# First loads of a two-layer backbone kernel: two small transfers issued by ScalarE, and eight products on a tile of ones ahead of the first projections

## The chip, the cores and the metric

One Trainium2 chip; the kernel runs on one core, in one launch. The metric is the device time of the launch in microseconds (us). Three runs of the kernel before gave 1178.02, 1180.78 and 1184.63 us; the median is 1180.78 us. One further execution was profiled.

## The reference

A two-layer backbone over 256 latent and 256 context tokens of width 1024, in float32. Every sub-layer is modulated by shift, scale and gate vectors that come from the conditions c and c_ctx. Layer 0 mixes tokens by bidirectional retention, layer 1 by neighbourhood attention; each is followed by a SwiGLU. What matters here is the very start:

```
cond_lat = silu(c);  cond_ctx = silu(c_ctx)
m = split(cond @ ada_w[i] + ada_b[i], 6)          # shift, scale, gate, ... per stream
a = h * (1 + m[1]) + m[0]                         # modulate
q, k, v, g = split(a @ ret_w_in, ...)             # first projections of layer 0
```

## The kernel before

All matrix products are made in float32 precision: mostly as three products on operands split into a high and a low part of type fp32r (`mm3`, L138 to L142). Only the first projections of head 0 start on whole, unsplit float32 operands, so that they need not wait for the split.

The start is written out by hand. `tc.manual_schedule(engines=REG)` (L372 to L424) fixes the order of TensorE (PE), VectorE (DVE), ScalarE (ACT), GpSimd (POOL) and SyncE (SP) in the order of the code. Past it, engines outside later hand-ordered regions take their order from the planner that builds the program on simulated times (`schedule_with_timeline_sim=True`). In the hand-ordered stretch:

- `load_cond` (L162 to L168): SP loads c, spread over all 128 partitions, into `condb[0]`, and c_ctx as a column tile `ccol` (128x8). ACT applies SiLU to both, `ccol` first.
- `load_adab` (L182 to L187): SP loads the adaLN biases `adab_sb` (128x96); POOL adds 1 to the columns of the scales.
- `ada.load_to(2)`, `load_x(0)`, `stream.load_to(1)`: SP loads the first two 512 KB tiles of the transposed adaLN weights (`adaraw`), the first 256 KB tile of tokens (`xt`, the inputs transposed) and the first 512 KB unit of projection weights (`raw`).
- `spread_cond` (L170 to L180): DVE splits `ccol` into `chi` and `clo`; PE spreads them over all partitions by 16 products with the identity, into two PSUM banks; ACT copies the two banks to `condb[1]`.
- Then a loop over eight row blocks kt of the model width. SP loads the next tiles; DVE makes scale and shift columns of kt for each of the two token streams s by multiply-and-sum over `adaraw` and `condb[s]` (L225, 128x1024, two for each kt and s); ACT writes the modulated tokens `am` (L408, 128x256) and their high part (L413); PE multiplies `am` with the unit. For kt below 5 that is `whole_products` (L345 to L354): for each s, four products into the banks of q and k and two into the banks of v, each of which the profile shows as two records. For kt from 5 on the products are split ones (`split_products`, L356 to L369).

PE takes its instructions in the order of the code, so what stands ahead of `whole_products` runs ahead of it. The eight PSUM banks are handed out in turn: two to `spread_cond`, then four for q and k, then four for v.

Of the kernel before, what the change touches and what calls it, by code (L numbers as in the profile page):

```python
# [10 lines left out]
BF16 = mybir.dt.bfloat16  # L11
# [7 lines left out]
P = 128  # L19
D = 1024  # L20
# [24 lines left out]
def backbone(ctx: ExitStack, tc: tile.TileContext, wpack, adapack, cond, condcol, xT, xtok, adab, lncol, lnrow,  # L45
             decay, delta, rope, rpb, mask8, out):
    nc = tc.nc
# [31 lines left out]
    def bank(name):  # L79
        return psum.tile([P, 512], F32, tag="bank", name=name)  # L80
# [75 lines left out]
    adab_sb = const.tile([P, 2, 48], F32, name="adab_sb")  # L156

    ccol = const.tile([P, KT], F32, name="ccol")
# [3 lines left out]
    def load_cond():  # L162


        nc.sync.dma_start(condb[0], cond[0:1, :].partition_broadcast(P))
        nc.sync.dma_start(ccol, condcol)
        nc.scalar.activation(ccol, ccol, AF.Silu)
        nc.scalar.activation(condb[0], condb[0], AF.Silu)  # L168

    def spread_cond():  # L170
        nc.vector.tensor_copy(out=chi, in_=ccol)
        nc.vector.tensor_tensor(out=clo, in0=ccol, in1=chi.bitcast(F32), op=ALU.subtract)
        for half in range(2):
            b = bank(f"cond_{half}")
            for i in range(4):
                k = 4 * half + i
                for n, c in enumerate((chi, clo)):
                    nc.tensor.matmul(b[:, i * P:i * P + P], c[:, k:k + 1].to_broadcast([P, P]), identr,
                                     start=i == 0 and n == 0, stop=i == 3 and n == 1)
            nc.scalar.copy(condb[1][:, half * 512:half * 512 + 512], b)  # L180

    def load_adab():  # L182
        nc.sync.dma_start(adab_sb, adab)
        for l in range(2):
            for g in (1, 4):
                sl = adab_sb[:, l, 8 * g:8 * g + 8]
                nc.gpsimd.tensor_scalar(out=sl, in0=sl, scalar1=1.0, scalar2=0.0, op0=ALU.add, op1=ALU.add)  # L187
# [129 lines left out]
    with Phase("ret", "yTh", "yTl", "vh", "vl", "kh", "kl") as rp:  # L317
# [12 lines left out]
                                      name=f"adaraw{i}")  # L330
# [42 lines left out]
        region = tc.manual_schedule(engines=REG)  # L373
        region.__enter__()
        load_cond()
        load_adab()
        ada.load_to(2)

        for i, w in enumerate("qk"):
            stream.place[16 * RET_H - 4 + i] = (rp, w + "h", w + "l", 1)  # L380
        load_x(0)
        stream.load_to(1)
        spread_cond()
        qk_ps = [bank(f"qk0_{f}") for f in range(4)]
        v_ps = [bank(f"v0_{t}") for t in range(4)]
        for kt in range(KT):
# [591 lines left out]
    with Phase("na", "oTh", "oTl", "qs") as ap:  # L978
# [196 lines left out]
        warm = ap.tile([P, 1], F32, name="warm")  # L1175
# [240 lines left out]
```

## Time and profile before

| | |
|---|---|
| median of three runs | 1180.78 us |
| the profiled execution, its own time | 1181.89 us |
| its span, first to last instruction | 1180.1 us |
| PE busy | 1153.0 us (98% of the span) |
| DVE, ACT, POOL busy | 67%, 39%, 25% |
| bytes moved by DMA | 201.72 MB, mean 171 GB/s |

The time of a row counts from the start of the span. PE's records overlap, since products are pipelined: the distance from one start to the next is the pace, not the length of a record. PEld is the loading of the stationary operand. SPq is SyncE's queue, which issues the transfers.

### The profile page before, as it was taken

Reading aid. Unit: us, or ns where it says so; the run is one execution under the profiler, and the core shown is the slowest. Engines: PE = TensorE matmul, PEld = TensorE weight load, DVE = VectorE, ACT = ScalarE, POOL = GpSimd, SP = SyncE. Lnnn points to the kernel's source line nnn. Section 1 sums busy time; section 2 is a strip of 40 time slices with the busy share of each in tenths; the row PEclk is TensorE's granted clock in tenths of the full one; section 3 lists DMA queues with packets and bytes.
Section 4 is the critical chain, followed back from the end, with each engine's and each line's share of the span. In section 5 each row is a group of like instructions: output and inputs, shape, how many; then the busy total and the mean of one; then the engine's idle time right before and its main releaser. Section 6 shows DMA issues by size and latency. Waiting matters only on the chain. (4 is left out here: it accounts for less than half of the span.)

```text
span 1180.1 us, 15314 instructions
## 1 busy us (share of the span) xinstructions
PE 1153.0 (98%) x5670; PEld 959.7 (81%) x5670; DVE 785.8 (67%) x1131; ACT 454.8 (39%) x714; POOL 293.8 (25%) x282
## 2 busy tenths in 40 slices
PE   7999999999999999999999999999998998999997
PEld 5778888888888888888888888887887877888886
DVE  7986957645745588857776576556265577788645
ACT  3582423332433252322122322244254465566530
POOL 0054114104203549100320000026244435300000
PEclk9999999999999999999999999999999999999999
DMA  8755464233434223566555586426587744777650
GB/s 328 262 202 190 175 206 150 90 126 129 133 107 127 88 72 108 181 145 226 178 192 209 168 271 234 139 66 136 160 233 226 204 141 121 238 237 228 206 167 36
DMA packets 70010, 201.72 MB, mean 171 GB/s; under 512 B 14512, under 2 KB 17072, under 8 KB 69936
## 3 DMA queue, kind: packets, MB, share of 16 engines
q1 hardware_dynamic: 69648, 200.23, 53.2%
q8 instruction: 44, 0.72, 0.3%
q10 hardware_dynamic: 288, 0.52, 0.1%
q14 instruction: 30, 0.25, 0.1%
HBM read 187.98 MB, written 2.25 MB: 161 GB/s over the span
## 5 line engine op out<-in xcount | busy, mean ns | idle before, releaser
L124 DVE TENSOR_TENSOR wlo<-raw,whi 128x1024 fp32r<-128x1024 f32 x220 | 291.9, 1332 | 210.6 <-ACT whi L123 204.0
L123 ACT CAST whi<-raw 128x1024 fp32r<-128x1024 f32 x220 | 229.5, 1048 | 457.5 <-PE f L141 118.1
L225 DVE CUSTOM_DVE_ANT_0 junk<-adaraw,cond,adab_sb 128x1024 bf16<-128x1024 f32 x160 | 219.1, 1369 | 46.9 <-DMA adaraw<-in_adapack 44.5
L141 PE MATMUL f<-aT,whi 128*128 128x512 f32 (+1 forms) x384 | 142.8, 372 | 1.8 <-DVE aT L756 1.7
L142 PE MATMUL f<-aT,wlo 128*128 128x512 f32 (+1 forms) x384 | 142.5, 371 | 0.0
L140 PE MATMUL f<-aT,whi 128*128 128x512 f32 (+1 forms) x384 | 142.5, 372 | 0.0
L857 PE MATMUL f<-aT,whi 128*128 128x512 f32 x320 | 112.9, 397 | 0.0
L313 POOL TENSOR_TENSOR pb_n<-pa_n,mhalf 128x1 f32<-128x1 f32 x12 | 8.4, 704 | 347.8 <-DVE pa_n L312 347.8
L858 PE MATMUL f<-aT,wlo 128*128 128x256 f32 x320 | 90.0, 282 | 0.3 <-DVE wlo L124 0.3
L141 PEld LDWEIGHTS f<-aT,whi 128*128 128x128 f32 x384 | 72.3, 188 | 14.6 <-DVE aT L756 1.9
L142 PEld LDWEIGHTS f<-aT,wlo 128*128 128x128 f32 x384 | 72.3, 188 | 12.6
L140 PEld LDWEIGHTS f<-aT,whi 128*128 128x128 f32 x384 | 72.3, 188 | 12.4
L857 PEld LDWEIGHTS f<-aT,whi 128*128 128x128 f32 x320 | 60.0, 188 | 14.4
L140 PE MATMUL d<-whi,hh 128*128 128x512 f32 x176 | 68.6, 389 | 0.0
L142 PE MATMUL d<-whi,hl 128*128 128x512 f32 x176 | 68.5, 389 | 0.0
L141 PE MATMUL d<-wlo,hh 128*128 128x512 f32 x176 | 68.5, 389 | 0.0
L142 PE MATMUL v<-whi,aT 128*128 128x512 f32 x160 | 62.5, 392 | 1.8 <-POOL aT L756 1.8
L140 PE MATMUL v<-whi,aT 128*128 128x512 f32 x160 | 62.5, 391 | 0.0
L622 POOL TENSOR_TENSOR z<-t,z 128x512 f32<-128x512 f32 x28 | 44.3, 1600 | 72.8 <-DVE t L620 72.6
L141 PE MATMUL v<-wlo,aT 128*128 128x512 f32 x160 | 62.3, 389 | 0.0
L858 PEld LDWEIGHTS f<-aT,wlo 128*128 128x128 f32 x320 | 60.3, 189 | 0.8 <-DVE wlo L124 0.7
L140 PE MATMUL g<-aT,whi 128*128 128x512 f32 x128 | 50.2, 392 | 2.3 <-ACT qf0q L493 2.3
(287 smaller groups left out, 2429.8 us busy)
## 6 DMA issues: line engine op xcount, KB each, us to landing
raw<-in_wpack SPq DMA_DIRECT2D x228, 512.0 KB, 3.6
adaraw<-in_adapack SPq DMA_DIRECT2D x96, 512.0 KB, 4.5
ln<-in_lnrow SPq DMA_DIRECT2D x16, 256.0 KB, 4.7
braw<-in_rpb SPq DMA_DIRECT2D x8, 512.0 KB, 5.3
kh<-sth SPq DMA_DIRECT2D x32, 128.0 KB, 2.5
kl<-stl SPq DMA_DIRECT2D x32, 128.0 KB, 2.4
gateb<-gscr SPq DMA_DIRECT2D x6, 512.0 KB, 6.4
xt<-in_xT SPq DMA_DIRECT2D x8, 256.0 KB, 4.6
```

The source lines that it names most:

```text
L123: nc.scalar.copy(hi, raw)
L124: self.last_low = nc.vector.tensor_tensor(out=lo, in0=raw, in1=hi.bitcast(F32), op=ALU.subtract)
L140: nc.tensor.matmul(o, s[0], m[0], start=start, stop=False)
L141: nc.tensor.matmul(o, s[0], m[1], start=False, stop=False)
L142: nc.tensor.matmul(o, s[1], m[0], start=False, stop=stop)
L225: nc.vector.tensor_tensor_reduce(out=junk, in0=self.tiles[i], in1=condb[s], scale=1.0, scalar=adab_sb[:, l, m:m + 1], op0=ALU.mult, op1=AL ...
L313: nc.gpsimd.tensor_tensor(out=b, in0=a, in1=mhalf[:, 0:n], op=ALU.pow)
L622: eng.tensor_tensor(out=z[t][:, cs], in0=t2, in1=z[t][:, cs], op=ALU.add)
L857: nc.tensor.matmul(b[i].rearrange("p (a t) -> p a t", a=2), st[0], m, start=kt == 0, stop=False)
L858: nc.tensor.matmul(b[i][:, 0:NLAT], st[1], m[:, 0, :], start=False, stop=kt == KT - 1)
```

## The change

ScalarE issues the loads of `ccol` and `adab_sb`, ahead of its own work; SyncE issues neither any more. VectorE sets a 128x512 tile of ones in bf16, and PE makes eight products on it (128x128 by 128x512) into a PSUM bank of their own that nobody reads, behind the 16 products that spread the condition and ahead of the first products on tokens.

```diff
     def load_cond():
+        nc.scalar.dma_start(ccol, condcol)
+        nc.scalar.dma_start(adab_sb, adab)
         nc.sync.dma_start(condb[0], cond[0:1, :].partition_broadcast(P))
-        nc.sync.dma_start(ccol, condcol)
         nc.scalar.activation(ccol, ccol, AF.Silu)
         nc.scalar.activation(condb[0], condb[0], AF.Silu)
 
-    def spread_cond():
+    def spread_cond(rp):
+        warm = rp.tile([P, D], BF16, tag="g3", name="warm")
+        nc.vector.memset(warm[:, 0:512], 1.0)
+        idle = bank("idle")
         nc.vector.tensor_copy(out=chi, in_=ccol)
         nc.vector.tensor_tensor(out=clo, in0=ccol, in1=chi.bitcast(F32), op=ALU.subtract)
         for half in range(2):
...
             nc.scalar.copy(condb[1][:, half * 512:half * 512 + 512], b)
 
+        for _ in range(8):
+            nc.tensor.matmul(idle, warm[:, 0:P], warm[:, 0:512], start=True, stop=True)
+
     def load_adab():
-        nc.sync.dma_start(adab_sb, adab)
         for l in range(2):
...
-        spread_cond()
+        spread_cond(rp)
```

## Rows read from the trace of the kernel before

**Rows 1.** The page of the profile, its parts 1 and 2: busy time of each engine with its share of the span, and the granted TensorE clock in 40 equal slices, in tenths.
```profile
PE 1153.0 (98%) x5670; PEld 959.7 (81%) x5670; DVE 785.8 (67%) x1131; ACT 454.8 (39%) x714; POOL 293.8 (25%) x282
...
PEclk9999999999999999999999999999999999999999
```

**Rows 2.** The waits of PE over the whole span: who waited for whom, us in total, times, longest.
```profile
PE cond L178 <- DVE chi L171: 5.2, 1, 5.2
PE o L1115 <- ACT pt L1105: 3.2, 1, 3.2
PE g L140 <- ACT qf0q L493: 2.3, 1, 2.3
...
PE qk L351 <- ACT am L408: 1.4, 1, 1.4
```

**Rows 3.** Stretches of the span: busy us (and instructions) of each engine, granted clock, share of the DMA engines that was busy, GB/s. These three cover all that follows 13.85 us.
```profile
13.85:600.00 586.15, 581.77 (x2717) 481.86 (x2716) 418.16 (x561) 206.99 (x297) 168.83 (x131) 1.00 0.47 158
600.00:1000.00 400.00, 392.21 (x1977) 322.77 (x1975) 238.92 (x387) 157.77 (x269) 106.30 (x128) 1.00 0.59 179
1000.00:1180.00 180.00, 171.81 (x956) 148.74 (x955) 121.80 (x173) 84.56 (x141) 15.99 (x9) 0.98 0.59 184
```

**Rows 4.** The timeline of PE at the start: start, us, line, operation and how many of them were merged into the row; in brackets the idle time ahead of it and what ended it.
```profile
5.20 0.44 PE L178 MATMUL cond<-identr,chi 128*128 128x128 f32 x1 [5.20 <-DVE chi L171]
5.45 0.42 PE L178 MATMUL cond<-identr,clo 128*128 128x128 f32 x1
...
8.23 0.41 PE L178 MATMUL cond<-identr,chi 128*128 128x128 f32 x1
8.44 0.41 PE L178 MATMUL cond<-identr,clo 128*128 128x128 f32 x1
10.30 3.72 PE L351 MATMUL qk<-am,raw 128*128 128x256 f32 x8 [1.44 <-ACT am L408]
13.85 1.88 PE L354 MATMUL v<-raw,am 128*128 128x512 f32 x4
15.57 1.89 PE L351 MATMUL qk<-am,raw 128*128 128x256 f32 x8
17.30 1.88 PE L354 MATMUL v<-raw,am 128*128 128x512 f32 x4
```

**Rows 5.** The tile raw from 0 to 16 us: its loads into the array (ns, least, median, most; first and last start), and the time from issue to landing of its transfers.
```profile
L351 PEld LDWEIGHTS qk<-am,raw x11: 190/332/338, 10.3 to 15.8; 128*128 128x128 f32 x11
...
DMA to landing us min/median/max: 6.5/8.8/9.6
```

**Rows 6.** The timeline of SP's queue: start, us, line, the tile and where it is loaded from.
```profile
0.72 0.38 SPq L165 DMA_DIRECT2D cond<-in_cond  x1
1.16 0.42 SPq L166 DMA_DIRECT2D ccol<-in_condcol  x1
1.63 0.42 SPq L183 DMA_DIRECT2D adab_sb<-in_adab  x1
2.10 0.91 SPq L217 DMA_DIRECT2D adaraw<-in_adapack  x2
3.04 0.43 SPq L336 DMA_DIRECT2D xt<-in_xT  x1
3.52 0.45 SPq L109 DMA_DIRECT2D raw<-in_wpack  x1
```

**Rows 7.** Stretches of the start, columns as in rows 3.
```profile
2.00:3.25 1.25, 0.00 (x0) 0.00 (x0) 0.00 (x0) 0.00 (x0) 0.40 (x2) 1.00 0.95 339
3.25:4.50 1.25, 0.00 (x0) 0.00 (x0) 0.00 (x0) 0.00 (x0) 0.00 (x0) 1.00 0.78 175
4.50:8.80 4.30, 3.60 (x16) 3.49 (x16) 2.12 (x5) 1.74 (x3) 0.90 (x4) 1.00 1.02 402
...
10.30:13.85 3.55, 3.55 (x8) 2.82 (x9) 3.44 (x7) 1.22 (x2) 0.00 (x0) 1.00 1.03 411
```

**Rows 8.** The timeline of ACT at the start.
```profile
0.72 1.28 ACT L167 ACT_TABLE_LOAD   x1 [0.72 <-PEq L1408]
4.65 0.21 ACT L167 ACTIVATE ccol<-ccol 128x8 f32<-128x8 f32 x1 [2.65 <-DMA ccol<-in_condcol]
4.76 1.04 ACT L168 ACTIVATE cond<-cond 128x1024 f32<-128x1024 f32 x1
...
8.89 0.59 ACT L180 COPY cond<-cond 128x512 f32<-128x512 f32 x1 [1.12 <-PE cond L178]
9.64 0.60 ACT L408 ACTIVATE am<-xt,ada 128x256 f32<-128x256 f32 x1 [0.17 <-DVE ada L225]
12.41 0.60 ACT L408 ACTIVATE am<-xt,ada 128x256 f32<-128x256 f32 x1 [2.17 <-DVE ada L225]
...
15.07 0.60 ACT L408 ACTIVATE am<-xt,ada 128x256 f32<-128x256 f32 x1 [1.41 <-DVE ada L225]
```

**Rows 9.** The timeline of DVE at the start.
```profile
4.89 0.17 DVE L171 CAST chi<-ccol 128x8 fp32r<-128x8 f32 x1 [4.89 <-ACT ccol L167]
...
6.98 1.29 DVE L225 CUSTOM_DVE_ANT_0 junk<-adaraw,cond,adab_sb 128x1024 bf16<-128x1024 f32 x1 [1.73 <-DMA adaraw<-in_adapack]
```

**Rows 10.** The timeline of POOL at the start.
```profile
0.93 0.42 POOL L445 MEMSET dp<- 128x384 f32 x1
...
2.10 0.29 POOL L261 CAST identr<-ident 128x128 fp32r<-128x128 f32 x1
5.19 0.90 POOL L187 TENSOR_SCALAR adab_sb<-adab_sb 128x8 f32<-128x8 f32 x4 [2.79 <-DMA adab_sb<-in_adab]
```

**Rows 11.** Transfers issued in the first 10 us: tile, queue, count, KB each, median us from issue to landing.
```profile
adab_sb<-in_adab SPq DMA_DIRECT2D x1, 48.0 KB, 3.5
ccol<-in_condcol SPq DMA_DIRECT2D x1, 4.0 KB, 3.5
```

**Rows 12.** The timeline of PE at two products with 512 columns, later on.
```profile
48.39 0.39 PE L368 MATMUL qk<-aT,whi 128*128 128x512 f32 x1
48.62 0.39 PE L369 MATMUL qk<-aT,wlo 128*128 128x512 f32 x1
```

**Rows 13.** The waits of SP's queue over the whole span, columns as in rows 2.
```profile
SPq L109 <- DVE wlo L124: 592.0, 147, 18.0
...
SPq L109 <- PE v L354: 21.0, 4, 5.9
```

## The prediction

> **What bounds the kernel now.** I read the page first: TensorE is busy for 98% of the span, no other engine above 67% [rows 1]. So the time is TensorE's list of products plus the gaps in it, and the second view is who makes TensorE wait. The longest wait of all is the first: 5.2 us until VectorE has `chi`; 1.4 us more stand ahead of the first tokens [rows 2]. Behind 13.85 us the three stretches leave 586.15 - 581.77, 400 - 392.21 and 180 - 171.81 us idle, 20.4 us in 1166 [rows 3]. The change touches only what stands ahead of that, so the third view is TensorE's timeline there.
>
> It shows 16 spreading products from 5.20 to 8.85, nothing for 1.44 us, then the first eight records on tokens in 3.55 us (10.30 to 13.85). The same eight records take 1.73 us the next time (15.57 to 17.30) [rows 4]. That is 0.444 against 0.215 us each, a factor of two, with no idle between. The loads into the array tell the same: 190 ns at best, 338 at worst [rows 5]. So the first eight ran at the lower of the two clock levels (1.2 GHz) and the later ones at the upper (2.4 GHz). The granted clock reads 1.00 throughout, at the start too [rows 1, 7]; it does not show this, and I go by the pace. What running low costs before is 3.55 - 1.72 = 1.83 us, and that is all a warmer start can give back.
>
> **Does a microsecond at the front reach the end?** Yes, nearly whole. SP's queue stands 592 us in waits on VectorE's splits and 21 us on products of the first stage [rows 13]: buffers come free as work is done, so the transfers follow TensorE. A start that is x earlier moves all of it by x.
>
> **The loads, part one.** SP issues `ccol` and `adab_sb` at 1.16 and 1.63 us and the first `adaraw` at 2.10 [rows 6]. Without the two, everything behind them on SP is issued 2.10 - 1.16 = 0.94 us earlier. What that is worth lies between nothing and 0.94: from 4.50 to 8.80 the DMA engines are busy throughout (1.02, 402 GB/s), so tiles there land as bytes go through, not as they are issued; only from 3.25 to 4.50 is there slack (0.78, 175 GB/s) [rows 7]. The last thing that the first products need is `raw`, issued at 3.52 and landing 6.5 us later, at 10.0 [rows 5, 6], right before they start at 10.30. I take half, 0.5 us: the two small loads must still pass through the same engines.
>
> The Trainium skill speaks against more (DMA: Bandwidth & Descriptors, "Issuing engines are not separate DMA queues"): whichever engine starts a transfer, it runs on the same 16 DMA engines, and a second issuer saves the issue time only. By that the gain is at most the 0.94 us above; the trace agrees so far as its DMA engines are full.
>
> **The loads, part two.** ScalarE issues `ccol` as its first instruction, at 0.72 instead of 1.16, where SP's first row is now [rows 6]; with 3.5 us to land [rows 11] that is 0.44 us earlier. ScalarE's own work hides both issues (0.42 us each by SP's rows): it has only the table load to 2.00 ahead of the SiLU at 4.65 [rows 6, 8]. The identity that the spread needs is ready at 2.39 [rows 10]. So SiLU, `chi` and the spread move 0.44 us ahead, to 4.76 until about 8.2 for the last start (8.44 + 0.215 - 0.44) [rows 4, 9]. `adab_sb` is issued about 1.14 instead of 1.63; POOL's four adds on it end by 6.1 now, ahead of the first sum at 6.98 [rows 9, 10]. Nothing waits there unless it lands over 0.9 us later.
>
> **The ones.** VectorE idles until 4.89, so the memset (POOL sets 128x384 in 0.42 us) is free [rows 9, 10]; without that cover it would hold `chi`, and so the spread, by as much. The bank of its own pushes the others on by one in turn: two banks of v wait, as now, for ScalarE's copies of the spread (the last ends at 9.48), and one for the products on ones, which stand ahead on TensorE anyway [rows 8].
>
> **The eight products on ones, the main term.** No row shows a bf16 product. Products with 512 columns follow at 0.23 us each at the upper level (48.39 to 48.62) [rows 12]; the records on tokens, with nearly that pace at the upper level (0.215), took 0.444 at the lower [rows 4]. So they end at 8.2 + 1.8 = 10.0 us or at 8.2 + 3.55 = 11.75, and nothing on tokens can start earlier, since TensorE keeps its order. The first `am`, now at 10.24 [rows 8], will be there between 9.3 and 10.2. The tokens therefore start where the ones end, never earlier than 10.0: part one of the loads is hidden under the ones.
>
> When does the clock rise? Before, it rose 3.55 us after work took up at 10.30 [rows 4]; the 3.65 us of spreading products ahead of the gap had not raised it by then. Two ends follow:
> - counted from the start of the spread, 4.76 + 3.55 = 8.3: all ones run at the upper level, tokens start at 10.0 and their first eight records end at 10.0 + 1.72 = 11.75. Gain 13.85 - 11.75 = 2.1 us.
> - counted from the first product on ones, 8.2 + 3.55 = 11.75: the ones run low, the eight records high, and end at 13.47. Gain 0.4 us.
>
> The work is now unbroken from the spread on, and nothing tells the ends apart, so I take the middle, 1.2 us. Next to be late is `am` of the second stream, ready at 13.01 [rows 8]: in the best case TensorE asks for it at 11.75 + 1.72 = 13.5, 0.5 us behind it. The next row block's (15.67) would be asked for at 16.9. So VectorE takes nothing back.
>
> **Sum.** -1.2 us. Against the profiled execution (1181.89 us: 1180.1 of span and 1.8 around it) that is 1180.7; it stands 1.1 above the median, so against 1180.78 it is 1179.6 us. The runs before lie 6.6 us apart; 0.5% of this kernel, 5.9 us, is about what a measurement can tell from no change.
>
> **The rivals.**
> - *The clock rises behind the ones.* The ones then only delay: they end at 11.75 and the eight records take 3.55 once more, to 15.3, where it was 13.85. That is 1.45 us slower, 1182.2. It decides where the rise comes after some 12.6 us: with two of the eight records low they end at 13.47 + 2 x 0.229 = 13.9. For it: 3.65 us of spreading were not enough before, and its records are no wide ones. Against it: no gap any more, and 3.55 us without one were enough. 0.15. The Trainium skill (TensorE: Matmul & The Clock Gate, "What's actually happening") holds that the same kernel has more or fewer slow products from run to run, so this may differ between runs; a single trace can't show it.
> - *`ccol` comes later, not earlier.* If ScalarE issues behind its table load, at 2.00 instead of 1.16 [rows 6, 8], the spread ends 0.84 us later, and the ones end at 11.3 to 13.0: the eight records end at 13.0 to 14.8, a gain of 0.8 or a loss of 0.9. No change, 1180.8. 0.10.
> - *The planner orders something else, worse.* Past the hand-ordered start some engines' order comes from simulated times, which the change moves. A swap that puts two or three waits like the 2.3 and 3.2 us ones [rows 2] into TensorE's list costs 5 to 9 us: 1188, slower by over 0.5%. It decides from the first swapped split of weights that a product waits for. Against it: the start's shift moves all that follows alike. 0.07.
> - *The same, better.* The same swaps can take such waits out of the 20.4 idle us [rows 3]: 1173. 0.08.
>
> **How the numbers follow.** The main case has 0.60, between a gain of 2.1 and of 0.4 us, so 1178.7 to 1180.4, and some 3 us of spread between runs on either side: 1175.7 to 1183.4 by itself. The first two rivals lie in that or a little above it. The last two reach past it by half of their weight each; with them the range is 1174.5 to 1185.0. Faster by over 0.5% is the last rival alone, 0.08; slower by over 0.5% the one ahead of it, 0.07; the rest, 0.85, lies within.
>
> **What the changed profile would show.** Right: the spread starts near 4.8 us; eight products on ones follow it without a gap; their pace goes from 0.44 to 0.22 us somewhere among them; the first eight records on tokens start between 10.0 and 11.8 us and take about 1.72. TensorE's work on tokens at 17.30 now is then found 0.4 to 2.1 us earlier, and the span's end as well. Wrong: first records at 0.44 us each, the spread later than 5.2, a gap ahead of the tokens longer than 0.3 us (the transfers then set the start), or a shift at 17.30 that the end doesn't show. A change of more than 6 us with a shift of 1 or 2 us at the start would mean another order of work later on.

## The result, and the profile after

The changed kernel's median is 1184.86 us (1183.16 to 1185.51, five runs) against 1180.78 (1178.02 to 1184.63, five runs): a ratio of 1.0038, 95% interval 1.0021 to 1.0055. Here and below the ratio comes from all runs of both kernels and need not be the quotient of the medians. It is about 4 us slower where I forecast 1 us faster, and no run of it is as fast as the median before. The profiled execution took 1184.86 us, with a span of 1183.0: 2.9 us longer than the one before.

The start first, in the order in which things become late. Landings in the changed kernel (us from issue to landing at the end of a line), c (`cond`) and the two small transfers:

```profile
cond<-in_cond SPq DMA_DIRECT2D x1, 512.0 KB, 4.8
adab_sb<-in_adab ACTq DMA_DIRECT2D x1, 48.0 KB, 6.1
ccol<-in_condcol ACTq DMA_DIRECT2D x1, 4.0 KB, 4.9
```

The landing of c before:

```profile
cond<-in_cond SPq DMA_DIRECT2D x1, 512.0 KB, 3.7
```

ACT, POOL and DVE of the changed kernel:

```profile
0.72 0.42 ACTq L165 DMA_DIRECT2D ccol<-in_condcol  x1
...
5.68 0.21 ACT L168 ACTIVATE ccol<-ccol 128x8 f32<-128x8 f32 x1 [2.75 <-DMA ccol<-in_condcol]
...
10.41 0.60 ACT L414 ACTIVATE am<-xt,ada 128x256 f32<-128x256 f32 x1
```
```profile
7.33 1.90 POOL L193 TENSOR_SCALAR adab_sb<-adab_sb 128x8 f32<-128x8 f32 x4 [4.94 <-DMA adab_sb<-in_adab]
```
```profile
7.63 1.28 DVE L231 CUSTOM_DVE_ANT_0 junk<-adaraw,cond,adab_sb 128x1024 bf16<-128x1024 f32 x1 [1.33 <-POOL adab_sb L193]
```

`ccol` is issued 0.44 us earlier, as forecast, but takes 4.9 us where it took 3.5 [rows 11]: SiLU starts at 5.68, not 4.65 [rows 8]. The biases take 6.1 us, and POOL's adds begin at 7.33 where they ended by 6.1 [rows 10]; the first sum waits for them, to 7.63 instead of 6.98 [rows 9]. c itself, issued first on SP's queue both times, lands 1.1 us later too.

PE at the start of the changed kernel:

```profile
6.24 0.44 PE L182 MATMUL cond<-identr,chi 128*128 128x128 f32 x1 [6.24 <-DVE chi L175]
...
9.69 3.07 PE L187 MATMUL idle<-warm 128*128 128x512 bf16 x8
12.60 1.89 PE L357 MATMUL qk<-am,raw 128*128 128x256 f32 x8
14.32 1.88 PE L360 MATMUL v<-raw,am 128*128 128x512 f32 x4
16.04 1.89 PE L357 MATMUL qk<-am,raw 128*128 128x256 f32 x8
```

The ones fill PE without a gap and the eight records on tokens take 1.72 us, as forecast. Counted from the start of the spread they end after 14.32 - 6.24 = 8.08 us, where it was 13.85 - 5.20 = 8.65 [rows 4]: 0.57 us won. But the spread starts 1.04 late, so the tokens stand 0.47 us behind (16.04 against 15.57). That is small, and far from 4. The waits of PE show the rest (us in total, times, longest), and PE's timeline where the longest new one ends:

```profile
PE cond L182 <- DVE chi L175: 6.2, 1, 6.2
PE g L140 <- ACT qf0q L499: 6.2, 1, 6.2
...
PE o L1121 <- ACT pt L1111: 0.6, 1, 0.6
```
```profile
63.51 0.39 PE L375 MATMUL v<-whi,aT 128*128 128x512 f32 x1
70.06 0.80 PE L140 MATMUL g<-aT,whi 128*128 128x512 f32 x1 [6.17 <-ACT qf0q L499]
70.66 0.63 PE L141 MATMUL g<-aT,whi 128*128 128x512 f32 x1
71.08 0.63 PE L142 MATMUL g<-aT,wlo 128*128 128x512 f32 x1
...
73.58 0.40 PE L142 MATMUL g<-aT,wlo 128*128 128x512 f32 x1
73.81 0.39 PE L140 MATMUL g<-aT,whi 128*128 128x512 f32 x1
```

The wait ahead of the first product of g is 6.17 us, not 2.31 [rows 2]. Behind it the pace is 0.43 us, the lower clock level, until 73.6. From 63.50 to 74.00 the granted clock is 0.67, where it was 1.00 (columns as in rows 3). Before, then after:

```profile
63.50:74.00 10.50, 8.20 (x36) 6.62 (x36) 9.85 (x14) 8.81 (x15) 4.75 (x5) 1.00 0.87 302
```
```profile
63.50:74.00 10.50, 4.33 (x12) 3.18 (x11) 9.42 (x14) 8.04 (x14) 4.76 (x5) 0.67 0.69 216
```

Before, the first g started at 66.02. The shift can be followed on from there by first starts: 0.18 us at the last product ahead of the wait (63.51 against 63.33), 4.04 at the first g (70.06), 5.6 at the first S, 5.5 at the last one and at the first product of o (877.60 against 872.12), and 2.8 at e, the last stage (S: products of q and k in layer 0; o: the output of attention in layer 1). So a shift set at g reaches 870 us undiminished. Before:

```profile
L140 PE MATMUL S<-qh,kh x32: 279/338/398, 87.9 to 371.7; 128*128 128x512 f32 x16, 128*128 128x256 f32 x16
...
L140 PE MATMUL e<-whi,h1h x110: 274/389/404, 1110.6 to 1171.6; 128*128 128x512 f32 x66, 128*128 128x256 f32 x44
```

After:

```profile
L140 PE MATMUL S<-qh,kh x32: 279/338/398, 93.5 to 377.2; 128*128 128x512 f32 x16, 128*128 128x256 f32 x16
...
L140 PE MATMUL e<-whi,h1h x110: 274/389/404, 1113.4 to 1174.5; 128*128 128x512 f32 x66, 128*128 128x256 f32 x44
```

So 3.9 us are lost in the wait and 1.6 in the records at the lower level (nine distances from the first g take 3.75 us, where they took 2.18). The 2.6 that come back are the wait ahead of a later product of o, at 889.38 us before: 3.2 us in that one execution [rows 2] and 0.6 here. There ACT's copy stands behind a cast of weights that waits for a transfer. Before, then after:

```profile
887.52 1.04 ACT L123 CAST whi<-raw 128x1024 fp32r<-128x1024 f32 x1 [5.54 <-DMA raw<-in_wpack]
```
```profile
890.41 1.05 ACT L123 CAST whi<-raw 128x1024 fp32r<-128x1024 f32 x1 [3.69 <-DMA raw<-in_wpack]
```

No other execution shown below has the wait of o above 1.5, so the 2.9 between the two spans is too little for what g costs. The 5.6 may be too much: run 6 below has the copy in its old place and loses the 1.6 of lower clock all the same. The 3.9 of the wait is what the two traces give to the copy's place alone; the medians differ by 4.1, and by 3.3 in run 5.

**What ended the wait.** ACT from 64 to 70 us before, and then after:

```profile
64.66 0.56 ACT L149 CAST vh<-v 128x512 fp32r<-128x512 f32 x1
65.59 0.38 ACT L493 ACTIVATE qf0q<-qk 128x256 f32<-128x256 f32 x1 [0.37 <-DVE rm_0q L488]
65.87 1.07 ACT L149 CAST vh<-v 128x512 fp32r<-128x512 f32 x2
68.26 0.71 ACT L462 ACTIVATE dx<-dlt,lgw,lg 128x384 f32<-128x384 f32 x1 [1.32 <-POOL Dw L463]
```
```profile
64.81 1.52 ACT L149 CAST vh<-v 128x512 fp32r<-128x512 f32 x3
68.44 0.71 ACT L468 ACTIVATE dx<-dlt,lgw,lg 128x384 f32<-128x384 f32 x1 [2.11 <-POOL Dw L469]
69.05 0.69 ACT L468 ACTIVATE dx<-dlt,lgw 128x384 f32<-128x384 f32 x1
69.65 0.36 ACT L499 ACTIVATE qf0q<-qk 128x256 f32<-128x256 f32 x1
```

The first g needs the PSUM bank that ACT's copy `qf0q` empties. Before, that copy stood behind one cast of v; now the planner has put it behind three casts and behind the two exponentials dx of head 3. Those need buffers that POOL's sum Dw of head 2 reads, and that sum stands behind the store of an earlier Dw. POOL's timeline, after:

```profile
66.80 1.61 POOL L469 TENSOR_TENSOR Dw<-dx,dx 128x384 f32<-128x384 f32 x1 [2.79 <-DMA dscr<-Dw]
```

The exponentials start at nearly the same time in both (68.26 and 68.44). What moved is the copy, from ahead of that wait to behind it: 65.59 to 69.65, 4.06 us, which is g's 4.04. PE's own order is the same but for the ones. The copy isn't all that the planner moved: on ACT two casts of weights ahead of g, and behind 70 us some exponentials and two table loads, stand elsewhere too. PE's list of waits has no other new one.

### The profile page after: what moved, and what is told of

Read it like the earlier page. It is cut to its first block, busy times and chain, and to the rows that moved or that the text cites. A ratio compares the mean times of both kernels' runs of the same rounds, so it can differ in the third digit from the quotient of the medians.

```text
span 1183.0 us, 15336 instructions
## 1 busy us (share of the span) xinstructions
PE 1155.2 (98%) x5678; PEld 960.8 (81%) x5678; DVE 785.0 (66%) x1132; ACT 453.0 (38%) x712; POOL 293.4 (25%) x282
## 5 line engine op out<-in xcount | busy, mean ns | idle before, releaser
L863 PEld LDWEIGHTS f<-aT,whi 128*128 128x128 f32 x320 | 60.0, 188 | 14.4
```

The source lines that it names most:

```text
L863: nc.tensor.matmul(b[i].rearrange("p (a t) -> p a t", a=2), st[0], m, start=kt == 0, stop=False)
```

## The experiments

Each kernel was compared with the kernel before in the same series (medians of before 1180.3 us for runs 1 to 4, 1180.9 for 5 to 8 and 1181.1 for 9 to 11). "An edge" makes one instruction keep its place behind another in the planner's order; it adds no wait on another engine.

**1. The copy pinned ahead of the exponentials.** The changed kernel with one edge:

```diff
+            c0 = nc.scalar.activation(f[:, 0, NLAT:], ps[0][:, NLAT:], AF.Copy, scale=scale)
+            if (h, which) == (0, "q"):
+                tc.add_manual_dep(dx[(3, 0)].ins, c0.ins.name, mybir.DependencyInfo(
+                    mybir.DependencyClass.NoSync, mybir.DependencyReason.DATA), reason="pin")
...
```


> The changed kernel, with one edge of issue order more: ScalarE's two exponentials dx of decay table 3 stay behind its first copy of qf0q out of PSUM, as they stood in the kernel before. Theory A (the planner put that copy behind the two exponentials, which wait for GpSimd's add, which waits for a store; TensorE waits 6.2 us for the bank and its clock falls): the wait ahead of the first product of g is 2.3 to 3.3 us, the products behind it run at 0.23 us from the first, and the time is 4 to 5 us below the changed kernel, within 1.5 us of the kernel before. Theory B (the start itself is what costs: late small loads, eight products at the lower clock, and everything behind shifted): no change against the changed kernel, 1184 to 1185 us. Theory C (the difference lies in the wait of o around 930 us, which the two profiles have at 3.2 and 0.6 us and which may vary by itself): no steady relation, time between the two.

1181.19 us, ratio 1.0012 (1.0000 to 1.0023). The wait ahead of g is 3.1 us and products there still run low (three casts of v stay ahead of the copy), which I had not expected. The wait of o is at 889 us, not around 930. Most of the loss is gone by that edge alone.

**2. The reverse: the kernel before, with the copy put behind the exponentials.** The same edge the other way round, from dx of head 3 to the copy.

> The kernel before, with one edge of issue order: ScalarE's first copy of qf0q stands behind the two exponentials dx of decay table 3, as the planner put it in the changed kernel. Nothing of the start is touched. Theory A: the wait ahead of g grows from 2.3 to about 6.2 us, the first seven or eight products of g run at the lower clock, and the time is 4 to 5.5 us above the kernel before, about 1185 to 1186 us. Theory B: at most 0.5 us, since the start is the old one. Theory C: no change that lasts beyond 930 us.

1182.9 us, ratio 1.0019 (1.0008 to 1.0030); wait of g 4.9 us, nine records at the lower level. PE at g, and ACT ahead of it:

```profile
69.28 0.80 PE L140 MATMUL g<-aT,whi 128*128 128x512 f32 x1 [4.91 <-DVE vl L150]
```
```profile
67.58 0.71 ACT L464 ACTIVATE dx<-dlt,lgw,lg 128x384 f32<-128x384 f32 x1 [1.11 <-POOL Dw L465]
68.19 0.69 ACT L464 ACTIVATE dx<-dlt,lgw 128x384 f32<-128x384 f32 x1
68.79 0.36 ACT L495 ACTIVATE qf0q<-qk 128x256 f32<-128x256 f32 x1
```

Slower with nothing changed at the start, but by 2.6 us and not the 4 to 5.5 expected. The copy ends at 69.15 and VectorE's split `vl` of v, which the profile names as the last to come, at 69.23, so both stand at the end of this wait. POOL's sum took 0.99 us here, not 1.61, so that the exponentials start at 67.58, not 68.44. That doesn't explain why less is lost: the first S is at 93.3, almost as late as in the changed kernel (93.5), and the first product of o 5.2 us late where it was 5.5. Behind that, this execution has no wait of o.

**3. The loads alone** (all that makes the ones taken out):

> Only the first half of the change: ccol and adab_sb are issued by ScalarE, no products on ones. The planner keeps the first copy of qf0q ahead of the exponentials, one cast later than in the kernel before. Theory A: no long wait ahead of g (2.3 to 3 us). The small loads land about 1.0 us (ccol) and 2.1 us (adab_sb) later, as in the changed kernel's profile; the first sum waits for GpSimd until 7.6, the first products on tokens start near 11.0 instead of 10.3, at the lower clock: 0.7 to 1 us slower than before, 1181.5 to 1182.5 us. Theory B: the late loads are the main cost, 3 to 4 us slower, 1184 us.

1180.13 us, ratio 1.0003 (0.9991 to 1.0015). The spread starts at 6.32, as late as in the changed kernel, but the copy stands ahead of the exponentials, g waits 1.8 us and no record is low. The late start alone costs nothing that shows, where I had expected about 1 us.

**4. The ones alone** (both loads issued by SP as before):

> Only the second half of the change: eight products on ones, with both small loads on SyncE as before. The planner keeps the first copy of qf0q ahead of the exponentials, two casts later than in the kernel before. Theory A: ones start at 8.65, run at 0.43 us until the clock rises near 12, and end at 11.8 to 12.1; the first eight records on tokens take 1.72 us and end near 13.6, 0.2 to 0.4 us ahead of before; wait ahead of g 2.5 to 3.5 us; time within 1 us of the kernel before. Theory B: the ones cost what the change costs, 1184 us.

1180.44 us, ratio 0.9996 (0.9986 to 1.0007). The spread starts at 5.25; all eight ones run low (8.69 to 12.12) and so do the first four records on tokens: the rise comes at 13.8, not near 12 as expected. Here too the copy stays ahead of the exponentials (g waits 3.4 us). Neither half makes the planner put the copy behind them, both together do.

**5. The changed kernel once more, and 6. with ACT's order at this place as before.** Run 6 has four edges: cast of v, copy of q, two casts of v, exponentials. The rest is left to the planner.

> The changed kernel itself once more, on the chip on which the next three run. Theory A (a swapped issue order on ScalarE costs about 5.5 us at the first g: wait and lower clock): wait of 6 us ahead of g, low clock behind it, 3 to 4.5 us above the kernel before. Theory D (most of the 4 us is the difference between executions, a wait of o near 930 us that only some have): within 1.5 us of the kernel before.

> The changed kernel with ScalarE's order at the first evacuation pinned to that of the kernel before: first cast of v, copy of qf0q, two casts of v, then the exponentials. Theory A: the wait ahead of g is 2.3 to 2.6 us, so the clock stays up behind it as in the kernel before; what is left is the start, where the ones end near 13.1 and the first tokens are 0.5 to 0.8 us late: 0.5 to 1 us above the kernel before, 3 to 4 us below the changed one. Theory B (the start costs): as the changed kernel.

Unpinned 1184.23 us, ratio 1.0031 (1.0018 to 1.0043), wait of g 5.9; pinned 1181.24, 1.0001 (0.9991 to 1.0010). With the loads and the ones in place and the old order of five instructions kept on one engine, the loss is gone. The pinned kernel's PE, at g:

```profile
66.06 0.50 PE L140 MATMUL g<-aT,whi 128*128 128x512 f32 x1 [2.29 <-ACT qf0q L503]
66.40 0.40 PE L141 MATMUL g<-aT,whi 128*128 128x512 f32 x1
66.63 0.39 PE L142 MATMUL g<-aT,wlo 128*128 128x512 f32 x1
66.86 0.57 PE L140 MATMUL g<-aT,whi 128*128 128x512 f32 x1
67.22 0.63 PE L141 MATMUL g<-aT,whi 128*128 128x512 f32 x1
```

The wait is that of before to 0.02 us, yet the clock fell at 66.9, which it had not done before. So the fall is not set by the length of that wait alone.

**7. Ones from 1.44 us on.** Eight products on ones ahead of the spread and eight behind it, loads by SP, ACT's order pinned.

> Both small loads on SyncE as before; eight products on ones ahead of the spreading products as well as the eight behind them; ScalarE's order pinned as in the run above. Work on TensorE is then unbroken from about 1.4 us on. Theory A: the clock rises between 4.9 and 8 us, the ones behind the spread end near 10.0 to 10.6, the first eight records on tokens take 1.72 us and end at 11.9 to 12.4, 1.5 to 1.9 us ahead of before; wait ahead of g 2.3 to 2.6 us; time 1 to 2 us below the kernel before. Theory B': a start that is earlier doesn't carry (DVE or the transfers set the pace by 60 us): the lead is gone at the first g, no change of time.

1180.64 us, 0.9997 (0.9982 to 1.0011). PE at its start:

```profile
1.44 3.60 PE L175 MATMUL idle<-warm 128*128 128x512 bf16 x8 [1.44 <-DVE warm L172]
5.58 0.44 PE L183 MATMUL cond<-identr,chi 128*128 128x128 f32 x1 [0.55 <-DVE chi L176]
...
9.03 3.64 PE L188 MATMUL idle<-warm 128*128 128x512 bf16 x8
12.46 2.65 PE L359 MATMUL qk<-am,raw 128*128 128x256 f32 x8
14.95 1.88 PE L362 MATMUL v<-raw,am 128*128 128x512 f32 x4
```

With one gap of 0.55 us in 11 us of work, all 16 ones run at the lower level (3.43 us from start to start for the second eight), and the rise comes only among the first tokens, near 13.9, not between 4.9 and 8. g waits 4.1 us although the order is pinned: ACT reaches the first of the pinned casts only at 67.42. The 1 to 2 us expected are not there.

**8. Small loads first on SP.** SP issues `ccol` and `adab_sb` ahead of the 512 KB of c; no ones.

> No ones; SyncE issues ccol and adab_sb first, ahead of the 512 KB load of the condition. Theory L (the small loads landed later from ScalarE's queue because large transfers of the other queue were let onto the same DMA engines between them): here ccol lands 2.3 to 3 us after its issue and the spread starts before 4.5 us; adab_sb lands by 4.5 us. Rival M (any small transfer of 128 short rows takes 3.5 us or more wherever it stands): ccol lands 3.5 us after issue, at 4.2, and the spread starts at 4.8. Time within 0.8 us of the kernel before either way, since the first tokens wait for the 512 KB loads.

1183.28 us, 1.0010 (0.9998 to 1.0022): the median is 2.3 above that of before, but the interval takes in no change. SiLU of `ccol` starts at 2.38: ahead of the large transfers the 4 KB are there at once. But c is issued 0.9 us later and takes 5.0 to land, SiLU of c moves from 4.76 to 6.60, the first sum to 8.39 and the tokens to 11.70. The spread, now done by 6.6, was not what the tokens waited for.

**9 to 11. The copy and its sums put earlier.** VectorE's four products of q ahead of the split of weight unit 9, ACT's first copy of q ahead of the cast of unit 11: in the kernel before (9), with the ones added (10), and in the changed kernel (11).

```diff
+    LATE, marks = (11, 9), {}
...
-                nc.scalar.copy(hi, raw)
+                after(nc.scalar.copy(hi, raw), "copy" if u == LATE[0] else None)
...
+                after(self.last_low, "times" if u == LATE[1] else None)
```

`after` adds an edge behind the marked instruction.

> The kernel before with one edit: the rotary products of q (VectorE) and ScalarE's first copy of q out of its bank are put ahead of one split of weights each, so that the bank of head 0's first q comes free sooner. Theory that what the changed kernel loses is the wait of TensorE ahead of the first g: that wait, 2.3 us before and 6.2 us after the change, is at most 0.5 us, no product there runs at the lower clock, the first S starts near 87.9 - 2.3 = 85.6 us or earlier, and the time falls by 2 to 4 us: 1176.5 to 1178.8 by the median of before, 1180.6. Rival (the work that is put off comes back as another wait, of products on weight units 9 and 11): TensorE waits for a split at 60 to 75 us by as much, and the time stays within 1 us of before.

> The same edit with the eight products on ones and the loads left on SyncE. If the products on ones do not bring the clock's rise forward, this is within 1 us of the same edit alone (1176.5 to 1178.8); if they save 0.4 to 2.1 us at the start once nothing later hides it, it is that much faster than the edit alone.

> The changed kernel with the same edit. Theory of the order: the wait ahead of the first g falls from 6.2 to at most 0.5 us, the first S starts 5 to 8 us earlier than in the changed kernel (93.5 us), and the time is 1176.5 to 1179.5, 5 to 8 us under the changed kernel and within 1 us of the edit alone. Rival (the loads by ScalarE's queue cost the time by themselves): still 3 us or more over the edit alone.

9: 1177.77 us, 0.9978 (0.9963 to 0.9993). 10: 1177.53, 0.9971 (0.9956 to 0.9985). 11: 1178.15, 0.9976 (0.9965 to 0.9987). All three beat the kernel before, by about 3 us, and lie 6 to 7 under the changed kernel's medians of the other series. They lie together: what the change lost is gone, and neither its loads nor its ones add or save anything that shows. In run 9 PE goes from v to g without a wait, and ACT's copy stands at 63.78:

```profile
63.85 0.39 PE L377 MATMUL v<-whi,aT 128*128 128x512 f32 x1
64.20 0.50 PE L148 MATMUL g<-aT,whi 128*128 128x512 f32 x1
64.54 0.40 PE L149 MATMUL g<-aT,whi 128*128 128x512 f32 x1
```

The first S of run 9 is at 86.1 us, half a us later than expected, with a spread that starts a whole us late in this execution. The work put off did not come back as another wait: the list of PE's waits has none new. Run 11 still waits 1.3 us there (0.3 in run 10), more than expected, and stays high.

How much of the 3 us is g's wait, these traces show only in part. Run 11's first S is 0.3 us ahead of that of before; most of what its span is shorter by (1175.9 against 1180.1) is the wait of o, which only that execution of before has at 3.2. Run 6 is the better measure, with the order of before and no wait of o: against it the first S of runs 9 to 11 is 3.4, 4.5 and 1.9 us earlier, and the span 2.8, 4.5 and 1.9 us shorter.

All thirteen executions, us: first starts of the spread, of the products on tokens and of S; "rise" is where the pace changes, from the records that ran at either pace; "low at g" says whether products behind the wait of g ran at the lower level:

| kernel | spread | tokens | rise | wait of g | low at g | first S | median |
|---|---|---|---|---|---|---|---|
| before | 5.20 | 10.30 | 13.8 | 2.3 | no | 87.9 | 1180.8 |
| changed | 6.24 | 12.60 | 12.0 | 6.2 | yes | 93.5 | 1184.9 |
| 1 | 6.36 | 13.12 | 13.0 | 3.1 | yes | 90.6 | 1181.2 |
| 2 | 5.12 | 10.17 | 15.6 | 4.9 | yes | 93.3 | 1182.9 |
| 3 loads | 6.32 | 11.13 | 14.5 | 1.8 | no | 87.5 | 1180.1 |
| 4 ones | 5.25 | 12.12 | 13.8 | 3.4 | yes | 91.5 | 1180.4 |
| 5 changed | 6.57 | 13.44 | 14.4 | 5.9 | yes | 95.1 | 1184.2 |
| 6 pinned | 6.40 | 12.80 | 12.3 | 2.3 | yes | 89.5 | 1181.2 |
| 7 | 5.58 | 12.46 | 13.9 | 4.1 | yes | 91.8 | 1180.6 |
| 8 | 2.94 | 11.70 | 17.7 | 2.3 | yes | 91.8 | 1183.3 |
| 9 | 6.20 | 11.23 | 15.2 | none | no | 86.1 | 1177.8 |
| 10 | 5.48 | 11.87 | 11.3 | 0.3 | no | 85.0 | 1177.5 |
| 11 | 6.31 | 13.19 | 13.8 | 1.3 | no | 87.6 | 1178.2 |

One profile doesn't stand for a median: the first S of runs 4 and 7 is 3.6 and 3.9 us late, their executions took 1181.5 and 1182.0 us, and their medians are those of before. So a late first S doesn't give the median. But apart from run 8, whose start is its own, the three slowest medians are those with the copy behind the exponentials, and the three fastest those without a wait of over 1.3 us at g.

## Why the prediction was wrong

**The step that failed is the rival "the planner orders something else, worse".** I gave it 0.07 with the reason that "the start's shift moves all that follows alike". That is nearly true of running work, not of the planner: with both halves of the change, and with neither alone, it put one copy of ACT behind two casts and two exponentials more at 65 us. What tipped it in its simulated times is not on record. I had the place in front of me: 2.3 us ahead of g, ended by `qf0q` [rows 2], which says that this copy has no slack at all, so that whatever is put ahead of it goes straight to PE. Pinned back, the loss went (run 6); put behind without the change, 2.6 us of it came (run 2). The rival's price, 5 to 9 us for two or three waits, was too high for the 4 measured, and it took one wait, not several: 3.9 us more of it, and in these executions 1.6 of lower clock, which I had not priced. The sum's 1.2 us were not there at the start either, where the tokens came 0.47 late; but a start like that, with the copy in its old place, costs nothing that shows (runs 3, 4 and 6).

**The loads, part two: sign wrong.** Forecast 0.44 us earlier, measured 1.04 later at the spread. Six executions with the loads on ACT's queue have SiLU between 5.68 and 6.00; of the six with SP issuing them in the old order, five lie between 4.57 and 5.03 and one, run 9, at 5.64, where c was late too (4.7 us to land, not 3.7). So most of it goes with the queue, and some with the execution. The landing time of 3.5 us that I carried over belonged to its place in SP's queue, right behind c: it did not go along with the transfer. With the loads on ACT's queue c too took 4.8 to 5.1 us to land, and 3.7 to 4.1 in the five; whether the second queue does this, or the large loads that SP then issues earlier, was not separated. "Nothing waits there unless it lands over 0.9 us later": the biases did, by 2.1, and the first sum waited for them.

**The loads, part one** stayed hidden under the ones, as forecast, but the 0.5 us that I took for it was not there: SP issues `raw` at 2.75, not 3.52, and it lands 7.6 us after that instead of 6.5: at 10.35 where it was 10.0. The earlier issue bought no bytes earlier. That is in line with what the Trainium skill states (DMA: Bandwidth & Descriptors, "Issuing engines are not separate DMA queues"): transfers of all issuers share the 16 engines. The trace agrees so far as `raw`, issued 0.77 us earlier, landed 0.35 later; the small ones landed later still.

**The ones, the main term:** in the profiled pair 0.57 us from the start of the spread, inside the 0.4 to 2.1 but below the middle. Over the executions it isn't a gain. From the start of the spread to the second stretch of q and k it took 10.4, 11.3, 10.0 and 10.5 us without ones (before, runs 2, 3, 9) and 9.8, 10.2, 11.2, 10.8, 9.9, 9.8 and 10.6 with them (changed, runs 1, 4, 5, 6, 10, 11): means 10.5 and 10.3. The rise does come sooner with them, 5.8 to 8.6 us behind the start of the spread against 8.2 to 10.5; but they take 2.9 to 3.4 us themselves, which eats it. Neither end of the range is what the runs show: in these seven the rise came 5.8 to 8.6 us behind the start of the spread and 2.3 to 5.1 behind the first product on ones, not 3.55 behind either. In run 7 it had not come after 11 us of work with one short gap. The Trainium skill (TensorE: Matmul & The Clock Gate, "What's actually happening") has the number of slow products differ between runs of one kernel; the changed kernel agrees, with the rise at 12.0 in one execution and 14.4 in the next.

**The rival "`ccol` comes later"** happened, by another way than named (landing, not issue: it was issued at 0.72). Its price, within 1 us either way, held: the eight records end 0.47 late.

**"Does a microsecond at the front reach the end?"** Only as long as the order holds. From g on it did: 5.5 us at the last S and at o. Ahead of g, 0.47 us late at 16.04 is 0.18 at 63.5, since a wait of 0.33 us at 54 us before is gone. Run 3 is 0.75 late at 16.32 yet 0.4 early at the first S, since the planner has two casts and then the copy there, at 65.14: its order is worth more than the start's shift.

**Right:** the bound (PE), no gap ahead of the tokens, and, in kind, the last sentence of what to look for: more at the end than the start moved did mean another order of work later on. Its mark of 6 us was not reached; 4 were enough. Of the signs of being wrong two came: the spread later than 5.2 (6.24), and an end that doesn't show the start's shift.

## What to carry to other kernels

Where a planner orders engines on simulated times, any edit may reorder work far behind it, here 50 us: compare each engine's order before and after, and first at the waits of the bounding engine that are already there, since an instruction whose completion ends such a wait has no slack. Such a wait is also where the gain lies: the runs that put the bank's emptying a split or two earlier were 3 us faster, where the start gave nothing that shows. A transfer's time to land is a property of its place among other transfers, so it may not be kept when the queue is changed. One profiled execution can hold a wait of 3 us that the others lack (o): compare several before pricing by it.

## What the runs showed that I had not expected

- 4 KB issued first on an idle machine landed within 1.7 us (run 8: issued at 0.72, used at 2.38); the same 4 KB issued by ACT while SP issues 512 KB took 4.9 to 5.3 us, behind c's own landing at 4.8 to 5.1.
- Eight bf16 products on a tile of ones, the 16 of the spread and eight more on ones, 11 us with one gap of 0.55, all ran ahead of the rise (run 7). Whether the data (all ones) or something else holds the clock was not tried.
- The same 2.3 us of waiting ahead of g was followed by the upper level once (before) and by eight or nine records at the lower level twice (runs 6 and 8). A wait of 3.16 us, that of o before, was followed by the upper level too (granted clock 1.00 from 885 to 893 us, products behind it 0.23 us apart). What decides is open.
